# A hybrid decoder trunk on one core: the stick-breaking softplus through |z|, causal rows from the longest down, and memory heads that start after half of their queries

## The chip, the cores and the metric

The kernel runs on one core of one Trainium2 chip. The metric is device time in microseconds (us) of one execution; the times given are medians of several executions. A core has a matrix engine (PE, with its weight loads shown as PEld), a vector engine (DVE), a scalar engine (ACT), a general engine (POOL) and a queue engine (SP), which here issues the weight DMAs. Each engine works through its own instructions in order and waits on semaphores for the others.

## The reference

Two layers, each a half-step SwiGLU, a mixing block, and another half-step SwiGLU, with RMSNorm around each. The sequence has 512 rows of width 1024, and the memory has 256 rows. What matters here is the mixing block:

```python
# stick-breaking attention, 8 heads of width 64; z = q k^T / 8, mask: key < query
log_beta = log_sigmoid(z)
log_not = where(mask, log_beta - z, 0.0)              # = -softplus(z)
log_between = cumsum(log_not, reverse=True) - log_not
w = where(mask, exp(log_beta + log_between), 0.0)
o_sb = w @ v
# forgetting attention, 8 heads of width 64; c = cumsum(log_sigmoid(f_logit + b))
p = softmax(where(key <= query, z + c_query - c_key, -inf)); o_fx = p @ v
# memory attention, 4 heads of width 128
o_mem = softmax(q_mem k_mem^T * 128 ** -0.5) @ v_mem
merged = sigmoid(u@Wg_sb)*(o_sb@W_sb) + sigmoid(u@Wg_fx)*(o_fx@W_fx) + sigmoid(u@Wg_mem)*(o_mem@W_mem)
h = h + rmsnorm(merged @ w_out)
```

## The kernel before

Activations are kept transposed, as tiles of 128 features by 512 rows. Every float32 operand of a large product is split into a high part (an ACT copy that rounds) and a low part (a DVE subtraction), and `mm3` (L180 to L184) issues three matmuls: high by high, high by low, low by high. Weights arrive by DMA in a `raw` tile and are split the same way.

Work for PE comes from two kinds of source. The first is a queue of jobs, `Q`: each job is one projection or gate product, and its weights are loaded and split ahead of it. `Q.step(limit)` runs the next piece of the running job (three matmuls), and begins a new job only if its number is below the limit. `Q.until(n)` calls `step(n)` until it returns nothing, so it finishes a job that is already running, whatever its number. The second source are the heads, written as generators: a head issues its score matmuls, then yields `("wait", W)`, a guess of how long its softmax takes on ACT and DVE, then issues its transposes, yields another wait, and then issues the product with the values. `Q.weave(chain, limit)` keeps an assumed clock and fills the assumed waits with steps of jobs below the limit. When no job below the limit is left, the chain's next part follows at once and PE waits for the softmax itself. The framework's scheduler may still move single instructions within an engine's order.

In a layer's mixing block the jobs stand in this order before the change: memory queries 0 and 1 (`q_mem(0)`, tiles `qm` 0 and 1), memory queries 2 and 3 (`q_mem(1)`), then for the pairs of heads of the stick-breaking branch (p = 0 to 3) and of the forgetting branch (2, 3, 0, 1): `project` of the next pair (values `pv` for every second pair, queries `pq`, keys `pk`) and a `merge` job (gate product `pg`, branch product `pb`, a sigmoid on ACT and DVE). `run` finishes both memory queries, then weaves the four memory heads (scores `zm`, transposes `ptm`, values `pvm`) up to the mark `marks[0, 0]`, that is with the jobs `pv`, `pq` and `pk` of pair 0. Each memory head's scores are issued ahead of the previous head's transposes, and the wait between them is dropped. Then every pair of a branch gives two heads (j = 0 and 1), each woven up to the merge job of its pair, `marks["m", br, p]`.

A stick-breaking head (`stick_head`, scores `zs`, transposes `pts`, values `pvs`) works on four query blocks, i = 0 to 3, with 128, 256, 384 and 512 keys. For each it takes exp, a minimum with 2^62, and ln(1 + .) in `log1p_exp` (L170 to L172), then max(z, .) (L892), a reversed running sum (L894), a subtraction (L895) and exp (L896). The first transposes, `pts ... _0`, read all four blocks. A forgetting head (`zf`, `ptf`, `pvf`) does max, exp, reciprocal and a multiply per block. `forget_cumsum` (its transposes: `pfl`) makes the running sum of the forget gates once per layer.

Of the kernel before, what the change touches and what calls it, by code (L numbers as in the profile page):

```python
# [12 lines left out]
AF = mybir.ActivationFunctionType  # L13
ALU = mybir.AluOpType
# [3 lines left out]
P = 128  # L18
# [4 lines left out]
def kernel(  # L23
# [38 lines left out]
    nc = tc.nc  # L62
    _, S, D = x.shape
    M = mem.shape[1]
    L = w_in.shape[0]
    NT = S // P
    ND = D // P
    MT = M // P
    HD = 64
    NP = 4  # L70
    NH = 8
    HEAD_ROWS = ((slice(0, HD), slice(HD, P), 0), (slice(HD, P), slice(0, HD), 1))
    NMH = 4
# [94 lines left out]
    def log1p_exp(t, z, bias=0.0):  # L168

        nc.scalar.activation(t, z, AF.Exp, bias=bias)  # L170
        nc.vector.tensor_scalar(t, t, 2.0 ** 62, None, ALU.min)
        nc.scalar.activation(t, t, AF.Ln, bias=one_t[:t.shape[0]])  # L172
# [156 lines left out]
    def wpair(src, ktiles, c0, name, scale=None):  # L329

        return [Unit(src, k, min(4, ktiles - k), c0, 256, f"{name}_{k}", scale) for k in range(0, ktiles, 4)]
# [542 lines left out]

    def stick_head(q, k, vts, pj, j, ot, name):

        ptile = []
        pzs = [pbank("z", f"z{name}_{i}") for i in range(NT)]
        for i, pz in enumerate(pzs):
            nc.tensor.matmul(pz[:, i * P:(i + 1) * P], ident16[:], strict16, start=True, stop=False,  # L880
                             skip_group_check=True)
        for i, pz in enumerate(pzs):
            w = (i + 1) * P
            wp = max(w, 256)
            qs = slice(i * P, (i + 1) * P)
            for kk in (j, 2 + j):
                nc.tensor.matmul(pz[:, :wp], q[:, j, qs], k[:, kk, :wp], start=False, stop=(kk == 2 + j),
                                 skip_group_check=True)
            zr, t = pz[:, :w], tmp(f"t{name}_{i}")

            log1p_exp(t[:, :w], zr)
            nc.vector.tensor_tensor(t[:, :w], zr, t[:, :w], ALU.max)  # L892
            back = t[:, w - 1::-1]
            nc.vector.tensor_tensor_scan(back, one_t[:].broadcast_to([P, w]), back, 0.0, ALU.mult, ALU.add)  # L894
            nc.vector.tensor_tensor(t[:, :w], zr, t[:, :w], ALU.subtract)  # L895
            nc.scalar.activation(t[:, :w], t[:, :w], AF.Exp)  # L896
            ptile.append(t)
        yield ("pe", 1.5)
        yield ("wait", W_SB0)
        wt = transposed(ptile, name)  # L900
        yield ("pe", 1.1)
        yield ("wait", W_SB1)
        attend(pbank("mm", "pv" + name), j, vts, pj, wt, ot, name)
        yield ("pe", 1.2)
# [12 lines left out]
    def fox_head(q, k, vts, pj, j, qk, ot, name, ahead):  # L917

        rc = slice(0, 104 if j == 0 else P)
        ptile = []  # L920
        pzs = [pbank("z", f"z{name}_{i}") for i in range(NT)]
        for i, pz in enumerate(pzs):
            nc.tensor.matmul(pz[:, i * P:(i + 1) * P], ident16[:], causal16, start=True, stop=False,
                             skip_group_check=True)
        for i, pz in enumerate(pzs):
            w = (i + 1) * P
            wp = max(w, 256)
            qs = slice(i * P, (i + 1) * P)
            nc.tensor.matmul(pz[:, :wp], q[:, j, qs], k[:, j, :wp], start=False, stop=False, skip_group_check=True)
            nc.tensor.matmul(pz[:, :wp], qk[rc, 0, qs], qk[rc, 1, :wp], start=False, stop=True, skip_group_check=True)  # L930
            st = sb.tile([P, 2], F32, tag="st", bufs=8, name=f"st{name}_{i}")
            nc.vector.tensor_reduce(st[:, 0:1], pz[:, :w], AX.X, ALU.max, negate=True)
            p = tmp(f"p{name}_{i}")
            nc.scalar.activation(p[:, :w], pz[:, :w], AF.Exp, bias=st[:, 0:1], accum_out=st[:, 1:2])
            nc.vector.reciprocal(st[:, 1:2], st[:, 1:2])
            nc.vector.tensor_scalar(p[:, :w], p[:, :w], st[:, 1:2], None, ALU.mult)
            ptile.append(p)
        yield ("pe", 1.5)
        yield ("wait", W_FX0)
        tri = transposed(ptile, name)  # L940
        yield ("pe", 1.1)
        yield ("wait", W_FX1)
        ahead()
        attend(pbank("mm", "pv" + name), j, vts, pj, tri, ot, name)
        yield ("pe", 1.2)
# [73 lines left out]
    def mixing(l, src, ks, vs, dst):  # L1019
# [41 lines left out]
        def proj(key, un, scale):  # L1061
# [8 lines left out]
            else:  # L1070
# [3 lines left out]
                for r, ro, j in HEAD_ROWS:  # L1074
# [3 lines left out]
                    else:  # L1078
                        nc.gpsimd.tensor_copy(t[ro, j], t[r, j])

        def project(br, p):
            base = br * 1536
            if (br, p) == (1, FOX[0]):
                un = [Unit(w_in[l], k, min(3, ND - k), base + 1024 + p * P, 2 * P + NH, f"v{l}_{br}_{p}_{k}")
                      for k in range(0, ND, 3)]
                Q.add(un, lambda: v_gates(br, p // 2, un))
            elif p % 2 == 0:
                un = wpair(w_in[l], ND, base + 1024 + p * P, f"v{l}_{br}_{p}")
                Q.add(un, lambda: v_half(br, p // 2, un))
            for x, off, scale in (("q", 0, 0.125), ("k", 512, None)):  # L1090
                un1 = Unit(w_in[l], 0, ND, base + off + p * P, P, f"{x}{l}_{br}_{p}")
                marks[br, p] = Q.add([un1], lambda x=x, un1=un1, scale=scale: proj((x, br, p), un1, scale))
                if (br, p, x) == (1, FOX[0], "q"):
                    Q.add([], lambda: forget_cumsum(l, st["fl"], st))

        def merge(br, w_br, dp):

# [28 lines left out]

        for c in range(2):
            un = wpair(w_in[l], ND, 3080 + c * 256, f"qm{l}_{c}")
            marks["first"] = Q.add(un, lambda c=c, un=un: q_mem(c, un), src.ready(range(NT)) if c == 0 else None)
        project(0, 0)  # L1130
        heads = [(0, p) for p in range(NP)] + [(1, p) for p in FOX]
        for i, (br, p) in enumerate(heads):
            if i + 1 < len(heads):
                project(*heads[i + 1])
            marks["m", br, p] = merge(*((2, w_br_mem, i % NP) if br == 0 else (0, w_br_sb, i % NP)))
        for dp in range(ND // 2):
            merge(1, w_br_fox, dp)

# [9 lines left out]
        def run():  # L1148
            Q.until(marks["first"])
            for i in range(NT):  # L1150
                nc.sync.dma_start(hsave[i], hT[i][:])
            st["o", 2] = [blk("o", f"om{l}_{i}") for i in range(NMH)]

            def mems():
                gens = [mem_head(st["qm"][i], ks, vs, i, st["o", 2][i], f"m{l}_{i}") for i in range(NMH)]

                def part(g):
                    for kind, us_ in g:
                        yield (kind, us_)
                        if kind == "wait":  # L1160
                            return
                yield from part(gens[0])
                for i in range(NMH):
                    if i + 1 < NMH:
                        yield from ((k_, u_) for k_, u_ in part(gens[i + 1]) if k_ == "pe")
                    yield from gens[i]

            Q.weave(mems(), marks[0, 0])
            fx = {}
            for br in range(2):  # L1170
                st["o", br] = [blk("o", f"o{l}_{br}_{p}") for p in range(NP)]
                for at, p in enumerate(FOX if br else range(NP)):
                    Q.until(marks[br, p])
                    q, k = st["q", br, p], st["k", br, p]
                    vt = st["v", br, p // 2]
                    for j in range(2):
                        nm = f"{'sf'[br]}{l}_{p}_{j}"
                        ot = st["o", br][p]
                        if br == 0:
                            head = stick_head(q, k, vt, p % 2, j, ot, nm)  # L1180
                        else:
                            def pre(at, j):

                                if j == 2:
                                    at, j = at + 1, 0
                                p = FOX[at] if at < NP else None
                                if (p, j) not in fx and ("k", br, p) in st:
                                    fx[p, j] = fox_pre(st["q", br, p], st["k", br, p], j, 2 * p + j, st["cs"], f"{l}_{p}_{j}")

                            pre(at, j)  # L1190
                            head = fox_head(q, k, vt, p % 2, j, fx[p, j], ot, nm, lambda at=at, j=j: pre(at, j + 1))
                        Q.weave(head, marks["m", br, p])
                Q.until(marks["m", br, FOX[-1] if br else NP - 1])

        marks["run"] = run
        return marks
# [84 lines left out]
```

## Time and profile before

| | |
|---|---|
| median of 3 runs | 2488.55 us (2482.97 to 2490.67) |
| profiled execution, its own time | 2486.44 us |
| its span, first to last instruction | 2484.3 us |
| PE busy | 2441.4 us, 98% |
| DVE busy | 1542.6 us, 62% |
| ACT busy | 1143.5 us, 46% |
| mean granted PE clock | 0.996 |

Busy time of an engine is the time in which an instruction of it runs; for PE, consecutive matmuls overlap. Idle time of PE is what is left, and it is put down to what ended it. In the profile, tile names carry no numbers: `ts` is the softplus tile of any stick-breaking head, `pts` the transposes of any. The two layers' mixing blocks lie at about 400 to 835 us and 1632 to 2067 us of the span.

### The profile page before, as it was taken

Reading aid. Unit: us, or ns where it says so; the run is one execution under the profiler, and the core shown is the slowest. Engines: PE = TensorE matmul, PEld = TensorE weight load, DVE = VectorE, ACT = ScalarE, POOL = GpSimd, SP = SyncE. Lnnn points to the kernel's source line nnn. Section 1 sums busy time; section 2 is a strip of 40 time slices with the busy share of each in tenths; the row PEclk is TensorE's granted clock in tenths of the full one; section 3 lists DMA queues with packets and bytes.
Section 4 is the critical chain, followed back from the end, with each engine's and each line's share of the span. In section 5 each row is a group of like instructions: output and inputs, shape, how many; then the busy total and the mean of one; then the engine's idle time right before and its main releaser. Section 6 shows DMA issues by size and latency. Waiting matters only on the chain.

```text
span 2484.3 us, 30885 instructions
## 1 busy us (share of the span) xinstructions
PE 2441.4 (98%) x12154; PEld 2066.2 (83%) x12154; DVE 1542.6 (62%) x2259; ACT 1143.5 (46%) x1875; POOL 76.9 (3%) x124
## 2 busy tenths in 40 slices
PE   7999999999999999999999999999999999999998
PEld 7888889888888888888888888898888888888887
DVE  4364666778776544556643646768787765436465
ACT  4333355666555433333433333446675554333333
POOL 0000000000110000000000000000001100000000
PEclk9999999999999999999999999999999999999999
DMA  5343334122222523432423333442222224233332
GB/s 178 102 136 119 108 138 145 53 83 72 76 77 77 184 85 106 131 123 94 161 85 111 126 126 116 137 137 63 69 68 85 77 95 160 88 108 126 127 102 102
DMA packets 233298, 270.53 MB, mean 109 GB/s; under 512 B 8361, under 2 KB 188609, under 8 KB 233153
## 3 DMA queue, kind: packets, MB, share of 16 engines
q1 hardware_dynamic: 233056, 268.53, 33.7%
q8 instruction: 95, 1.56, 0.3%
q14 instruction: 51, 0.41, 0.0%
q0 software_dynamic: 96, 0.03, 0.0%
HBM read 262.24 MB, written 6.29 MB: 108 GB/s over the span
## 4 chain that ended last, share of the span: by engine, by line
PE 84%; DVE 8%; ACT 4%; DMA 2%; issue 1%; SPq 0%; DVEq 0%; ACTq 0%
PE pgc L183 3%; PE pgc L184 3%; PE pgc L182 3%; PE puc L183 3%; PE puc L184 3%; PE puc L182 3%; PE pga L183 3%; PE pga L184 3%; PE pga L182 3%; PE pua L184 3%; PE pua L183 3%; PE pua L182 3%; PE pg L182 3%; PE pg L184 3%; PE pg L183 3%; PE pdc L183 2%
## 5 line engine op out<-in xcount | busy, mean ns | idle before, releaser
L182 PE MATMUL pg<-us_a,wh_wg 128*128 128x512 f32 x384 | 150.4, 392 | 0.0
L184 PE MATMUL pg<-us_a,wl_wg 128*128 128x512 f32 x384 | 149.7, 390 | 0.0
L183 PE MATMUL pg<-us_a,wh_wg 128*128 128x512 f32 x384 | 149.6, 390 | 0.0
L182 PE MATMUL puc<-us_b,wh_uc 128*128 128x512 f32 (+1 forms) x384 | 142.6, 372 | 2.3 <-DVE fb L492 2.3
L184 PE MATMUL puc<-us_b,wl_uc 128*128 128x512 f32 (+1 forms) x384 | 142.4, 371 | 0.0
L183 PE MATMUL puc<-us_b,wh_uc 128*128 128x512 f32 (+1 forms) x384 | 142.4, 371 | 0.0
L182 PE MATMUL pgc<-us_b,wh_gc 128*128 128x512 f32 x320 | 124.5, 389 | 0.0
L183 PE MATMUL pgc<-us_b,wh_gc 128*128 128x512 f32 x320 | 124.5, 389 | 0.0
L184 PE MATMUL pgc<-us_b,wl_gc 128*128 128x512 f32 x320 | 124.5, 389 | 0.0
L163 DVE TENSOR_TENSOR wl_uc<-raw_uc,wh_uc 128x1024 fp32r<-128x1024 f32 x44 | 53.9, 1225 | 105.5 <-ACT wh_uc L162 105.5
L163 DVE TENSOR_TENSOR wl_ua<-raw_ua,wh_ua 128x1024 fp32r<-128x1024 f32 x44 | 53.9, 1225 | 96.5 <-ACT wh_ua L162 96.5
L163 DVE TENSOR_TENSOR wl_ga<-raw_ga,wh_ga 128x1024 fp32r<-128x1024 f32 x40 | 49.0, 1224 | 67.8 <-ACT wh_ga L162 67.8
L162 ACT CAST wh_uc<-raw_uc 128x1024 fp32r<-128x1024 f32 x44 | 46.3, 1052 | 92.5 <-PE pgc L183 39.4
L163 DVE TENSOR_TENSOR wl_gc<-raw_gc,wh_gc 128x1024 fp32r<-128x1024 f32 x40 | 48.9, 1223 | 63.4 <-ACT wh_gc L162 63.4
L184 PE MATMUL pda<-wh_da,ala 128*128 128x512 f32 x224 | 87.1, 389 | 0.0
L182 PE MATMUL pda<-wh_da,aha 128*128 128x512 f32 x224 | 87.1, 389 | 0.0
L183 PE MATMUL pda<-wl_da,aha 128*128 128x512 f32 x224 | 87.1, 389 | 0.0
L182 PE MATMUL pdc<-wh_dc,ahc 128*128 128x512 f32 x224 | 87.1, 389 | 0.0
L183 PE MATMUL pdc<-wl_dc,ahc 128*128 128x512 f32 x224 | 87.1, 389 | 0.0
L184 PE MATMUL pdc<-wh_dc,alc 128*128 128x512 f32 x224 | 87.1, 389 | 0.0
L162 ACT CAST wh_ga<-raw_ga 128x1024 fp32r<-128x1024 f32 x40 | 42.1, 1053 | 96.3 <-PE pua L183 76.3
L162 ACT CAST wh_ua<-raw_ua 128x1024 fp32r<-128x1024 f32 x44 | 46.2, 1051 | 86.7 <-PE pga L183 35.8
(437 smaller groups left out, 7285.6 us busy)
## 6 DMA issues: line engine op xcount, KB each, us to landing
raw_da<-in_ffn_w_down_dram SPq DMA_DIRECT2D x52, 512.0 KB, 3.3
raw_dc<-in_ffn_w_down_dram SPq DMA_DIRECT2D x52, 512.0 KB, 3.2
raw_wg<-in_w_gate_dram SPq DMA_DIRECT2D x48, 512.0 KB, 3.5
raw_ga<-in_ffn_w_gate_dram SPq DMA_DIRECT2D x44, 512.0 KB, 3.6
raw_ua<-in_ffn_w_up_dram SPq DMA_DIRECT2D x44, 512.0 KB, 3.6
raw_gc<-in_ffn_w_gate_dram SPq DMA_DIRECT2D x44, 512.0 KB, 3.6
raw_uc<-in_ffn_w_up_dram SPq DMA_DIRECT2D x44, 512.0 KB, 3.6
bta<-in_ffn_w_down_dram SPq DMA_DIRECT2D x16, 512.0 KB, 4.6
```

Source lines behind the costliest of these rows:

```text
L162: nc.scalar.copy(h_ap, src)
L163: nc.vector.tensor_tensor(l_ap, src, h_ap.bitcast(F32), ALU.subtract)
L182: nc.tensor.matmul(pt, lh, rh, start=start, stop=False, skip_group_check=free)
L183: nc.tensor.matmul(pt, lh, rl, start=False, stop=False, skip_group_check=free)
L184: nc.tensor.matmul(pt, ll, rh, start=False, stop=stop, skip_group_check=free)
```

## The change

Four things are changed in the mixing block. The softplus of a stick-breaking head becomes max(z, 0) + ln(1 + exp(-|z|)): ACT takes the absolute value, the exponential with scale -1 and the logarithm in a row, and DVE takes max and sum in one instruction; the minimum is gone. Both kinds of causal head issue and process their query blocks from i = 3 (512 keys) down to i = 0. The memory heads are woven in from the moment the first pair of memory queries is projected; each head asks, by `Q.until`, for the job with its own queries. And the value projections become jobs of their own, `project_v`, that stand behind the merge job of the pair two places earlier; a pair of heads may use all jobs up to the queries and keys of the pair after the next (`limits`), no longer only up to its own merge.

```diff
     def stick_head(q, k, vts, pj, j, ot, name):
-        for i, pz in enumerate(pzs):
+        for i in reversed(range(NT)):
+            pz = pzs[i]
...
-            log1p_exp(t[:, :w], zr)
-            nc.vector.tensor_tensor(t[:, :w], zr, t[:, :w], ALU.max)
+            nc.scalar.activation(t[:, :w], zr, AF.Abs)
+            nc.scalar.activation(t[:, :w], t[:, :w], AF.Exp, scale=-1.0)
+            nc.scalar.activation(t[:, :w], t[:, :w], AF.Ln, bias=one_t[:])
+            nc.vector.scalar_tensor_tensor(t[:, :w], zr, 0.0, t[:, :w], ALU.max, ALU.add)
...
     def fox_head(q, k, vts, pj, j, qk, ot, name, ahead):
-        for i, pz in enumerate(pzs):
+        for i in reversed(range(NT)):
+            pz = pzs[i]
...
+        def project_v(br, p):
+            base = br * 1536 + 1024 + p // 2 * 2 * P
+            if (br, p) == (1, FOX[0]):
+                un = [...]
+                Q.add(un, lambda: v_gates(br, p // 2, un))
+                Q.add([], lambda: forget_cumsum(l, st["fl"], st))
+            else:
+                un = wpair(w_in[l], ND, base, f"v{l}_{br}_{p}")
+                Q.add(un, lambda: v_half(br, p // 2, un))
         def project(br, p):
-            (the values' jobs)
+            marks["before", br, p] = len(Q.jobs)
             for x, off, scale in (("q", 0, 0.125), ("k", 512, None)):
                 marks[br, p] = Q.add([un1], lambda ...: proj((x, br, p), un1, scale))
-                if (br, p, x) == (1, FOX[0], "q"):
-                    Q.add([], lambda: forget_cumsum(l, st["fl"], st))
...
-            marks["first"] = Q.add(un, lambda c=c, un=un: q_mem(c, un), ...)
-        project(0, 0)
+            marks["qm", c] = Q.add(un, lambda c=c, un=un: q_mem(c, un), ...)
+        marks["first"] = marks["qm", 0]
+        project_v(*heads[0])
+        project(*heads[0])
-        for i, (br, p) in enumerate(heads):
+        for i, (br, _) in enumerate(heads):
             if i + 1 < len(heads):
                 project(*heads[i + 1])
-            marks["m", br, p] = merge(...)
+            merge(...)
+            if i % 2 == 0 and i + 2 < len(heads):
+                project_v(*heads[i + 2])
+        limits = [marks["before", *h] for h in heads[2:]] + 2 * [len(Q.jobs)]
...
             def mems():
+                def head(i):
+                    Q.until(marks["qm", i // 2])
+                    return mem_head(st["qm"][i], ks, vs, i, st["o", 2][i], f"m{l}_{i}")
...
+                gen = head(0)
+                yield from part(gen)
                 for i in range(NMH):
                     if i + 1 < NMH:
-                        yield from ((k_, u_) for k_, u_ in part(gens[i + 1]) if k_ == "pe")
-                    yield from gens[i]
+                        following = head(i + 1)
+                        yield from ((k_, u_) for k_, u_ in part(following) if k_ == "pe")
+                    yield from gen
+                    gen = following
...
-                        Q.weave(head, marks["m", br, p])
-                Q.until(marks["m", br, FOX[-1] if br else NP - 1])
+                        Q.weave(head, limits[br * NP + at])
+            Q.until(limits[-1])
```

More of the change, by code (lines that the diff above doesn't have):

```diff
@@ L875, in stick_head @@
     def stick_head(q, k, vts, pj, j, ot, name):
-        ptile = []
+        ptile = {}
         pzs = [pbank("z", f"z{name}_{i}") for i in range(NT)]
@@ L896, in stick_head @@
             nc.scalar.activation(t[:, :w], t[:, :w], AF.Exp)
-            ptile.append(t)
+            ptile[i] = t
         yield ("pe", 1.5)
@@ L919, in fox_head @@
         rc = slice(0, 104 if j == 0 else P)
-        ptile = []
+        ptile = {}
         pzs = [pbank("z", f"z{name}_{i}") for i in range(NT)]
@@ L936, in fox_head @@
             nc.vector.tensor_scalar(p[:, :w], p[:, :w], st[:, 1:2], None, ALU.mult)
-            ptile.append(p)
+            ptile[i] = p
         yield ("pe", 1.5)
@@ L1079, in proj @@
                         nc.gpsimd.tensor_copy(t[ro, j], t[r, j])
+        def project_v(br, p):
+            base = br * 1536 + 1024 + p // 2 * 2 * P
+            if (br, p) == (1, FOX[0]):
+                un = [Unit(w_in[l], k, min(3, ND - k), base, 2 * P + NH, f"v{l}_{br}_{p}_{k}")
+                      for k in range(0, ND, 3)]
+                Q.add(un, lambda: v_gates(br, p // 2, un))
[3 more added lines that the diff above has]
+                Q.add(un, lambda: v_half(br, p // 2, un))
         def project(br, p):
             base = br * 1536
[L1083 to L1089, printed above, removed]
+            marks["before", br, p] = len(Q.jobs)
             for x, off, scale in (("q", 0, 0.125), ("k", 512, None)):
@@ L1128, in mixing @@
             un = wpair(w_in[l], ND, 3080 + c * 256, f"qm{l}_{c}")
-            marks["first"] = Q.add(un, lambda c=c, un=un: q_mem(c, un), src.ready(range(NT)) if c == 0 else None)
-        project(0, 0)
+            marks["qm", c] = Q.add(un, lambda c=c, un=un: q_mem(c, un), src.ready(range(NT)) if c == 0 else None)
+        marks["first"] = marks["qm", 0]
         heads = [(0, p) for p in range(NP)] + [(1, p) for p in FOX]
-        for i, (br, p) in enumerate(heads):
+        project_v(*heads[0])
+        project(*heads[0])
+        for i, (br, _) in enumerate(heads):
             if i + 1 < len(heads):
                 project(*heads[i + 1])
-            marks["m", br, p] = merge(*((2, w_br_mem, i % NP) if br == 0 else (0, w_br_sb, i % NP)))
+            merge(*((2, w_br_mem, i % NP) if br == 0 else (0, w_br_sb, i % NP)))
+            if i % 2 == 0 and i + 2 < len(heads):
+                project_v(*heads[i + 2])
+        limits = [marks["before", *h] for h in heads[2:]] + 2 * [len(Q.jobs)]
         for dp in range(ND // 2):
@@ L1154, in mems @@
             def mems():
-                gens = [mem_head(st["qm"][i], ks, vs, i, st["o", 2][i], f"m{l}_{i}") for i in range(NMH)]
+                def head(i):
+                    Q.until(marks["qm", i // 2])
+                    return mem_head(st["qm"][i], ks, vs, i, st["o", 2][i], f"m{l}_{i}")
                 def part(g):
@@ L1161, in part @@
                             return
-                yield from part(gens[0])
+                gen = head(0)
+                yield from part(gen)
                 for i in range(NMH):
                     if i + 1 < NMH:
-                        yield from ((k_, u_) for k_, u_ in part(gens[i + 1]) if k_ == "pe")
-                    yield from gens[i]
+                        following = head(i + 1)
+                        yield from ((k_, u_) for k_, u_ in part(following) if k_ == "pe")
+                    yield from gen
+                    gen = following
             Q.weave(mems(), marks[0, 0])
```

## The prediction

> **What bounds the kernel now.** I read the page first, then PE's waits in the first mixing block, then that block cut at each place where PE stops.
>
> ```profile
> span 2484.3 us, 30885 instructions
> ...
> PE 2441.4 (98%) x12154; PEld 2066.2 (83%) x12154; DVE 1542.6 (62%) x2259; ACT 1143.5 (46%) x1875; POOL 76.9 (3%) x124
> ```
>
> PE is the bound: it idles 2484.3 - 2441.4 = 42.9 us in all. The built program of the changed kernel has the same 12154 matmuls in the same sizes, so the change can only move PE's stalls, and only in the two mixing blocks. The next view is busy time by stretch (us, then PE, PEld, DVE, ACT, POOL, granted PE clock), with its own total, for the first layer, and one stretch of the second.
>
> ```profile
> 458.00:467.00 9.00, 6.95 (x32) 5.13 (x32) 7.13 (x14) 5.01 (x14) 2.56 (x4) 0.81 0.21 60
> ...
> 498.00:504.00 6.00, 5.49 (x37) 4.45 (x36) 4.41 (x9) 4.29 (x10) 0.21 (x1) 1.00 0.50 159
> 504.00:533.00 29.00, 29.00 (x182) 26.18 (x181) 24.85 (x47) 19.22 (x39) 0.20 (x1) 1.00 0.22 64
> 533.00:536.00 3.00, 1.69 (x13) 1.35 (x12) 2.25 (x4) 1.78 (x4) 1.03 (x1) 1.00 0.48 143
> ...
> 582.00:589.00 7.00, 6.61 (x45) 5.32 (x43) 4.61 (x9) 4.46 (x10) 0.20 (x1) 1.00 0.55 157
> ...
> 617.00:620.00 3.00, 2.28 (x16) 1.84 (x15) 2.97 (x5) 1.59 (x4) 0.41 (x1) 1.00 0.00 0
> ...
> 774.00:776.00 2.00, 1.09 (x7) 0.77 (x6) 1.67 (x2) 2.00 (x6) 0.00 (x0) 1.00 0.78 257
> ...
> sum 422.00, PE 415.97 PEld 356.14 DVE 314.81 ACT 250.05 POOL 37.08; mean PE 32.00 PEld 27.40 DVE 24.22 ACT 19.23 POOL 2.85
> ...
> 1690.00:1699.00 9.00, 7.13 (x33) 5.45 (x31) 7.46 (x16) 5.24 (x12) 2.36 (x3) 0.81 0.19 59
> ```
>
> From 413 to 835 us PE idles 422.00 - 415.97 = 6.03 us, nearly all in the six places shown; the second layer repeats the first (1.87 us in the stretch that answers to the first row, 2.05 us there). The first row also shows a clock of 0.81, a loss of 9 x 0.19 = 1.7 us. So all there is to win is about 2 x (6.0 + 1.7) = 15.4 us, 0.6% of the time. The rows below say what ends each stop.
>
> ```profile
> 453.83 0.28 PE L184 MATMUL zm<-mk,qm 128*128 128x256 f32 x1
> 453.95 1.04 PE L978 MATMUL ptm<-ident,pm 128*128 128x128 f32 x8
> 454.75 0.48 PE L182 MATMUL pk<-us_a,wh_k 128*128 128x512 f32 x1
> ...
> 456.92 0.39 PE L182 MATMUL pvm<-ptm,mv 128*128 128x512 f32 x1
> ...
> 458.29 0.60 PE L978 MATMUL ptm<-ident,pm 128*128 128x128 f32 x4
> ...
> 460.27 0.44 PE L978 MATMUL ptm<-ident,pm 128*128 128x128 f32 x2 [1.28 <-DVE pm L969]
> 461.31 0.44 PE L978 MATMUL ptm<-ident,pm 128*128 128x128 f32 x2 [0.60 <-DVE pm L969]
> ...
> 462.37 0.79 PE L182 MATMUL pvm<-ptm,mv 128*128 128x512 f32 x1 [0.17 <-ACT ptm L162]
> ...
> 499.33 0.50 PE L858 MATMUL pvs<-pts,v 128*128 128x512 f32 x1 [0.51 <-ACT pts L162]
> ...
> 532.83 0.39 PE L184 MATMUL pg<-us_a,wl_wg 128*128 128x512 f32 x1
> 533.06 0.49 PE L871 MATMUL pts<-ident,ts 128*128 128x128 f32 x3
> 534.86 0.88 PE L871 MATMUL pts<-ident,ts 128*128 128x128 f32 x6 [1.31 <-ACT ts L896]
> ...
> 584.34 0.67 PE L858 MATMUL pvs<-pts,v 128*128 128x512 f32 x2 [0.29 <-DVE pts L163]
> ...
> 619.09 0.98 PE L871 MATMUL pts<-ident,ts 128*128 128x128 f32 x7 [0.72 <-ACT ts L896]
> ...
> 775.43 0.50 PE L858 MATMUL pvf<-ptf,v 128*128 128x512 f32 x1 [0.91 <-ACT ptf L162]
> ```
>
> Four kinds. At the **end of the memory heads** the queue below the limit is empty, and PE waits for the last head's softmax (1.28 + 0.60 + 0.17). In stick heads 1/1 and 3/1 (pair/j) the **last exp comes late** (1.31, 0.72). After heads 0/1 and 2/1 the merge's last three matmuls are all that covers the **split of the transposes** (the stretches at 498 and 582: 0.51 and 0.39). The end of the last forgetting head costs 0.91.
>
> **The change, part by part**, per layer.
>
> *Memory heads, +2.0 us.* At first sight the new weave gives them 48 more matmuls (`pqm` 2 and 3, 2 x 24). But each new head calls `Q.until`, which finishes whatever job is running. The order of the built program shows it: all 48 stand between the first head's scores and the second's, where the old order had 57 shorter ones (`pv`); then the rest of `pv` (39) is finished ahead of the third head's scores, and the rest of `pk` (18) ahead of the fourth's. So the queue is empty earlier: old, nine `pk` matmuls stand between the third head's transposes and its `pvm`; new, none do. In the rows, those nine run from 454.75 to 456.92, 2.17 us. The wait they cover is from the last score matmul (453.83) to the last `ptm` (461.31), 7.48 us, and its ACT and DVE work (max, exps, multiplies, the split of `ptm`, a gate weight, the keys) is the same in the new order. Take away 2.17 us of cover and PE idles 2.17 us more, part of it now ahead of `pvm`. I take +2.0. Ends: +0.5 if the key and weight splits, which now partly run earlier, shorten the wait; +3.9 if a second span of half clock (1.7) joins.
>
> *Softplus and row order: the late exps, 0.* The groups of all lines give the price of each step.
>
> ```profile
> L894 DVE TENSOR_TENSOR_SCAN ts<-one_t,ts 128x128 f32<-128x128 f32 (+1 forms) x64 | 50.0, 806 | 0.3
> ...
> L172 ACT ACTIVATE ts<-ts,one_t 128x128 f32<-128x128 f32 (+1 forms) x64 | 32.5, 555 | 5.0 <-DVE ts L171 4.8
> ...
> L896 ACT ACTIVATE ts<-ts 128x128 f32<-128x128 f32 (+1 forms) x64 | 30.1, 470 | 31.2 <-DVE ts L895 30.2
> ...
> L892 DVE TENSOR_TENSOR ts<-zs,ts 128x128 f32<-128x128 f32 (+1 forms) x64 | 28.9, 477 | 0.7 <-ACT ts L172 0.5
> ...
> L895 DVE TENSOR_TENSOR ts<-zs,ts 128x128 f32<-128x128 f32 (+1 forms) x64 | 28.8, 475 | 0.3
> ...
> L170 ACT ACTIVATE ts<-zs 128x128 f32<-128x128 f32 (+1 forms) x64 | 24.8, 436 | 1.2 <-PE zs L887 0.9
> ...
> L171 DVE TENSOR_SCALAR ts<-ts 128x128 f32<-128x128 f32 (+1 forms) x64 | 18.3, 317 | 0.5
> ```
>
> Removed: 64 minima, 18.3 us of DVE, and two crossings between ACT and DVE per block. Added: 64 absolute values, which no row shows; the nearest is L170, which reads the same scores (24.8 us), and the bounds are 18.3 (L171) and 32.5 us (L172). The exp now reads SBUF as L896 does (30.1 for 24.8), and the fused max and sum I price as L892. Per head (16 of them): ACT (24.8 + 32.5 + 30.1) / 16 = 5.5 becomes 7.3 us; DVE (18.3 + 28.9 + 50.0 + 28.8) / 16 = 7.9 becomes 6.7. In the row 504:533 DVE is busy 86% and ACT 66%, so the load goes from the fuller engine to the emptier one. All of this lies beside PE's matmuls; what counts is when the last exp is ready. Longest first, the last block is the short one, so less follows it, but the first transpose now needs it, while before only the fourth did (the row at 533.06 shows three going ahead).
>
> The program's order tells more. In the old order the matmuls that stand between a head's last exp and its `pts` are 17, 6, 19, 2, 8, 8, 16, 3 for heads 0/0 to 3/1; PE waits at those with 2 and 3, and at no other. In the new order they are 7, 6, 8, 6, 2, 11, 3, 10: again one 2 and one 3, at heads 2/0 and 3/0. I take the same price in the new places: 0 net. Ends: -2.0 (both gone: 1.31 + 0.72) and +2.0 (two more such heads).
>
> Here the Trainium skill speaks against the change: "ScalarE: Activation LUTs", section "Rules for kernel authors", wants maximum and the like on VectorE and not on ScalarE. The trace agrees on the price of one: 317 ns for the DVE minimum against 436 ns for the nearest ACT row. By that rule the swap would lose 64 x 0.119 = 7.6 us of engine time.
>
> *Value projections and limits, -0.7 us.* The limit of pairs 0 and 2 now takes in the following `pv` job, so their second heads get 33 `pv` matmuls ahead of `pvs` (old: three `pb`). The stops at 498 and 582 go, 0.90 us. In return pairs 1 and 3 end at their merge: three and six `pb` matmuls are left there. The first is the old case again (about 0.45), the second half covered (0.2), partly filled by the scheduler. I take -0.7 with the slower starts around each stop; ends -1.5 and 0. The `pv` weights are fetched and split one pair earlier on SP, ACT and DVE; no row shows PE waiting for a weight here, and the order of weights is otherwise kept. The `pfl` transposes move from head 3/1 to 3/0, behind the first block's subtraction as before: 0 to +0.5.
>
> *Forgetting heads, +0.4 us.* Same instructions, the long block first. Between the last multiply and the first `ptf` the order has 4 matmuls at heads 2/0 and 1/0 and 1 at 1/1 (old: 9, 5 and 0, but there the first three transposes could go ahead), so PE may stop briefly where it doesn't now. 0 to +1.2.
>
> Sum per layer: +2.0 + 0 - 0.7 + 0.4 = +1.7, twice +3.4. The profiled execution's own time is 2486.44 us (span 2484.3 and 2.1 around it), which makes 2489.8; it lies 2.1 us under the median of the runs, 2488.55. Set on the median: 2492.0 us.
>
> **Rivals.** *ACT becomes the bound of the stick heads* (slower). ACT's chain grows by 1.9 us a head. It decides where fewer than about nine matmuls (2 us) follow the last exp: six heads of eight. At half of 1.9 us in each, 2 x 6 x 0.94 = 11.3 us, which with the rest (+3.4) is 2503. For: these engines are in-order, and weight splits and sigmoids share them. Against: 66% against 86% above. By the rule of the Trainium skill quoted above this is how it goes. *The late exps go and the memory tail hardly grows* (small gain): 2 x (-2.0 - 0.7 + 0.4 + 0.5) = -3.6, 2485. For: two crossings and the DVE step less. *The tail shrinks so far that the half clock goes too* (faster): 2 x (-2.0 - 1.5 - 1.0 - 1.7) = -12.4, 2476. Against: the order, which empties the queue sooner. "TensorE: Matmul & The Clock Gate", Part 1, in the Trainium skill, has the clock judged in free-running windows of 3413 ns; 1.7 us lost at half rate is such a window, and the trace agrees. *The stalls only change places*: 2488.5.
>
> **How the numbers follow.** 0.3% is 7.5 us, about what a measurement of this kernel can tell from no change. My forecast (2492) has 0.45, stalls that only change places 0.13, the small gain 0.12, ACT as the bound 0.22, the fast case 0.08. The forecast's own upper end, with second half-clock spans in both layers, passes 2496: I move 0.04 of its chance there. Faster 0.08, same 0.66, slower 0.26. The range goes from 2482, between the small gain and the fast case (ends -2.0, -1.5, 0, +0.5 twice: -6.0), to 2503.
>
> **What would show it.** In the changed profile: PE idle ahead of `pvm` and the last `ptm` about 4 us per layer instead of 2.05; no `pvs` stop after heads 0/1 and 2/1; waits on the last exp at 2/0 and 3/0 and none at 1/1 and 3/1; ACT some 30 us busier, DVE some 18 us less. I am wrong if PE's waits on `ts` grow beyond 4 us a layer (ACT), or if the memory tail idles less than now.

## The result, and the profile after

| | before | changed |
|---|---|---|
| median, 22 runs each | 2486.45 us (2482.61 to 2490.76) | 2491.03 us (2488.12 to 2495.06) |
| ratio, 95% interval | | 1.0017 (1.0012 to 1.0023) |
| profiled execution, its own time | 2486.44 us | 2490.06 us |
| its span | 2484.3 us | 2487.9 us |

The change costs 0.17%, about 4.2 us (3.0 to 5.7), against a forecast of +3.4 us. The page of the changed kernel:

```profile
span 2487.9 us, 30833 instructions
...
PE 2443.4 (98%) x12154; PEld 2066.1 (83%) x12154; DVE 1525.5 (61%) x2195; ACT 1163.1 (47%) x1939; POOL 77.3 (3%) x124
```

PE's 12154 matmuls are the same, DVE is 17.1 us less busy and ACT 19.6 us more. Busy time by stretch (us; PE, PEld, DVE, ACT, POOL; granted clock; then the DMA engines' share and GB/s), the first layer and one stretch of the second:

```profile
454.00:465.00 11.00, 8.15 (x38) 6.75 (x37) 8.40 (x18) 6.28 (x16) 2.27 (x3) 0.69 0.17 48
...
545.00:549.00 4.00, 3.80 (x20) 2.56 (x19) 3.31 (x6) 3.69 (x8) 0.00 (x0) 1.00 0.66 209
...
561.50:564.50 3.00, 1.91 (x13) 1.37 (x12) 2.94 (x7) 2.37 (x6) 0.00 (x0) 1.00 0.00 0
...
603.00:611.00 8.00, 7.25 (x38) 5.54 (x37) 7.31 (x14) 4.37 (x10) 1.60 (x1) 1.00 0.50 133
...
617.00:620.00 3.00, 1.75 (x12) 1.42 (x11) 2.89 (x7) 0.77 (x2) 0.71 (x2) 1.00 0.56 178
...
774.00:778.00 4.00, 3.28 (x19) 2.40 (x18) 3.53 (x9) 3.67 (x9) 0.00 (x0) 1.00 0.43 131
...
sum 422.00, PE 415.06 PEld 354.57 DVE 304.51 ACT 257.74 POOL 37.13; mean PE 31.93 PEld 27.27 DVE 23.42 ACT 19.83 POOL 2.86
...
1690.00:1702.00 12.00, 9.15 (x49) 7.68 (x49) 8.58 (x18) 7.00 (x16) 2.27 (x3) 0.86 0.16 44
```

PE idles 422.00 - 415.06 = 6.94 us where it idled 6.03. At the end of the memory heads it is 2.85 us instead of 2.05, at a clock of 0.69 in the first layer: two half-clock spans, a loss of at most 11 x 0.31 = 3.4 us (part of them falls on idle time), before it was one. Over whole executions the clock does not explain the 4.2 us: the mean granted clock of the changed kernel's 22 runs is 0.9962, and that of the kernel before, in the three sets of 24 to 33 runs made beside the experiments, 0.9957 to 0.9960. The two profiled executions have five half-clock spans of 3.41 us each ahead of their last 15 us. The rows of PE say what ended each stop:

```profile
454.57 0.28 PE L184 MATMUL zm<-mk,qm 128*128 128x256 f32 x1
454.69 1.04 PE L983 MATMUL ptm<-ident,pm 128*128 128x128 f32 x8
456.02 0.50 PE L182 MATMUL pvm<-ptm,mv 128*128 128x512 f32 x1 [0.29 <-ACT ptm L162]
459.08 0.80 PE L183 MATMUL pvm<-ptm,mv 128*128 128x512 f32 x1 [2.56 <-DVE ptm L163]
...
462.34 1.06 PE L983 MATMUL ptm<-ident,pm 128*128 128x128 f32 x4
...
563.73 0.98 PE L871 MATMUL pts<-ident,ts 128*128 128x128 f32 x7 [1.09 <-ACT ts L900]
...
609.97 1.20 PE L871 MATMUL pts<-ident,ts 128*128 128x128 f32 x9 [0.53 <-ACT ts L900]
...
618.54 0.62 PE L858 MATMUL pvs<-pts,v 128*128 128x256 f32 x3 [1.25 <-DVE pts L163]
...
775.70 1.28 PE L871 MATMUL ptf<-ident,pf 128*128 128x128 f32 x10 [0.60 <-DVE pf L941]
```

The nine `pk` matmuls between the third `ptm` and its `pvm` are gone, and PE stands 2.56 us in front of the second `pvm` matmul until DVE has split the transposes. DVE is late with that split because the splits of a gate weight and of the new keys (and a maximum) stand ahead of it in its order. In the kernel before, the same split began 1.43 us after the start of the last `zm`, in the changed one 3.77 us after it; first the row of the kernel before, then those of the changed one:

```profile
455.26 0.69 DVE L163 TENSOR_TENSOR ptm<-ptm,ptm 128x512 fp32r<-128x512 f32 x1
```

```profile
454.89 1.23 DVE L166 SCALAR_TENSOR_TENSOR wl_wg<-raw_wg,wh_wg 128x1024 fp32r<-128x1024 f32 x1
456.04 0.68 DVE L163 TENSOR_TENSOR k<-pk,k 64x512 fp32r<-64x512 f32 x1
...
457.41 0.69 DVE L163 TENSOR_TENSOR k<-pk,k 64x512 fp32r<-64x512 f32 x1
...
458.34 0.69 DVE L163 TENSOR_TENSOR ptm<-ptm,ptm 128x512 fp32r<-128x512 f32 x1
```

The last group of `ptm` then starts without a wait. Heads 2/0 and 3/0 wait for their last exp (1.09, 0.53), 1/1 and 3/1 no longer do, and the stops of 0.5 us for `pvs` after 0/1 and 2/1 are gone. A stop of 1.25 us within `pvs` of head 3/0 is new. It ends with the split of the last transposes, and ahead of that split DVE works through `forget_cumsum` (tiles `fa`, `fb`, `cs`) and a weight, 4.7 us in all; this running sum came one head later in the old order:

```profile
613.29 0.67 DVE L1015 TENSOR_TENSOR fa<-fb,fa 8x512 f32<-8x512 f32 x1
613.99 1.22 DVE L1016 TENSOR_TENSOR_SCAN fb<-one_t,fa 8x512 f32<-8x512 f32 x1
615.13 1.19 DVE L163 TENSOR_TENSOR wl_q<-raw_q,wh_q 128x1024 fp32r<-128x1024 f32 x1
616.35 1.68 DVE L1021 TENSOR_TENSOR cs<-fb,cs 8x512 fp32r<-8x512 f32 x2
618.07 0.62 DVE L163 TENSOR_TENSOR pts<-pts,pts 128x256 fp32r<-128x256 f32 x2
```

### The profile page after: what moved, and what is told of

It reads as the page before. It is cut to its first block, busy times and chain, and to the rows that moved or that the text cites. A ratio compares the mean times of both kernels' runs of the same rounds, so it can differ in the third digit from the quotient of the medians.

```text
span 2487.9 us, 30833 instructions
## 1 busy us (share of the span) xinstructions
PE 2443.4 (98%) x12154; PEld 2066.1 (83%) x12154; DVE 1525.5 (61%) x2195; ACT 1163.1 (47%) x1939; POOL 77.3 (3%) x124
## 4 chain that ended last, share of the span: by engine, by line
PE 85%; DVE 7%; ACT 4%; DMA 3%; issue 1%; SPq 0%; DVEq 0%; ACTq 0%
PE puc L183 3%; PE puc L184 3%; PE puc L182 3%; PE pgc L183 3%; PE pga L183 3%; PE pgc L182 3%; PE pga L182 3%; PE pg L184 3%; PE pgc L184 3%; PE pg L183 3%; PE pg L182 3%; PE pga L184 3%; PE pua L182 3%; PE pua L184 3%; PE pua L183 3%; PE pdc L183 2%
```

## The experiments

Two theories stood at the start. A: PE's stops decide, and `Q.until` in the new memory heads takes their cover away. B: ACT's longer chain in the stick heads is the loss. Each part was run alone on the kernel before; memory, softplus and row order were then left out of the changed kernel one by one; and the call of `Q.until` was mended. The ratios of the experiments (7 to 11 runs each) are to runs of the kernel before made beside them, with medians of 2485.43 to 2485.93 us, not to the 2486.45 in the first row; differences given below in us are differences of these ratios. The last column is read from the starts of matmuls in each trace: the stretch from the first `pqm` matmul to the last `pb` of the forgetting branch, in layer 1 and layer 2, and in brackets how many half-clock spans of 3.41 us (at most 1.7 us lost in each) lie in it.

| run | median us | ratio to before, 95% | mixing stretch, us |
|---|---|---|---|
| before | 2486.45 | 1 | 440.4, 440.3 (1, 1) |
| changed | 2491.03 | 1.0017 (1.0012 to 1.0023) | 443.4, 442.1 (2, 1) |
| mem_only | 2489.07 | 1.0016 (1.0007 to 1.0025) | 440.1, 440.0 (0, 0) |
| softplus_only | 2490.13 | 1.0021 (1.0013 to 1.0030) | 442.5, 442.2 (1, 1) |
| order_only | 2488.84 | 1.0015 (1.0006 to 1.0024) | 440.0, 441.6 (0, 1) |
| values_only | 2485.12 | 0.9997 (0.9988 to 1.0006) | 439.8, 438.5 (1, 0) |
| softplus_and_order | 2492.83 | 1.0026 (1.0016 to 1.0036) | 444.3, 442.7 (1, 0) |
| all_but_memory | 2488.82 | 1.0010 (1.0001 to 1.0019) | 441.3, 441.2 (1, 1) |
| all_but_softplus | 2492.75 | 1.0026 (1.0017 to 1.0036) | 444.7, 443.7 (2, 1) |
| all_but_order | 2487.51 | 1.0005 (0.9996 to 1.0013) | 440.5, 439.3 (1, 0) |
| until_mended | 2481.68 | 0.9986 (0.9977 to 0.9995) | 438.5, 438.4 (0, 0) |
| mended_memory_only | 2480.18 | 0.9979 (0.9970 to 0.9989) | 437.8, 437.7 (0, 0) |
| values_and_mended_memory | 2482.16 | 0.9986 (0.9977 to 0.9995) | 438.4, 437.3 (1, 0) |
| mended_all_but_order | 2478.42 | 0.9972 (0.9961 to 0.9983) | 436.7, 436.8 (0, 0) |

### One part at a time

mem_only, on the kernel before:

```diff
+        marks["first"] = marks["qm", 0]
...
+                def head(i):
+                    Q.until(marks["qm", i // 2])
+                    return mem_head(st["qm"][i], ks, vs, i, st["o", 2][i], f"m{l}_{i}")
...
```

> Memory heads alone changed (Q.until in each new head, start after half of the queries); softplus, row order, values and limits as before. Theory A (the call of Q.until burns the cover, and this is what makes the changed kernel slower): PE waits about 2.6 us for the low part of ptm ahead of the third pvm in each layer, the stick heads' waits stay as before (1.31 and 0.72 us on the last exp at heads 1/1 and 3/1), and the kernel is slower by 2 x 2 = 4 us, up to 6 with one more half-clock span, ratio 1.0016 to 1.0024. Theory B (the loss comes from ACT in the stick heads, the new weave gives the memory heads more cover): same or faster, ratio 0.998 to 1.000.

softplus_only:

```diff
-            log1p_exp(t[:, :w], zr)
-            nc.vector.tensor_tensor(t[:, :w], zr, t[:, :w], ALU.max)
+            nc.scalar.activation(t[:, :w], zr, AF.Abs)
+            nc.scalar.activation(t[:, :w], t[:, :w], AF.Exp, scale=-1.0)
+            nc.scalar.activation(t[:, :w], t[:, :w], AF.Ln, bias=one_t[:])
+            nc.vector.scalar_tensor_tensor(t[:, :w], zr, 0.0, t[:, :w], ALU.max, ALU.add)
```

> Only the softplus changed (Abs, Exp, Ln on ACT, max and sum in one on DVE). Theory A: the stalls only change places; the program's order has the last exp 2 to 4 matmuls ahead of pts at heads 1/0, 2/0 and 3/0 and no longer at 1/1 and 3/1, so 0 to 1 us per layer either way: ratio 0.9995 to 1.0005. Theory B (ACT is the bound): waits on the last exp grow to over 4 us a layer, ratio 1.002 or more. ACT busier by 20 to 30 us, DVE less by about 18 us in both.

order_only, in both kinds of causal head:

```diff
-        for i, pz in enumerate(pzs):
+        for i in reversed(range(NT)):
+            pz = pzs[i]
```

> Only the order of the query blocks changed (512 keys first) in both kinds of causal head. Theory A: waits on the last exp move from heads 1/1 and 3/1 (2.0 us together) to 0/0, 2/0 and 3/0 (about 1.5 us together), and the forgetting heads get 0.4 to 0.6 us of waits for ptf per layer: ratio 0.9997 to 1.0006. Theory B: neutral as well. A third theory (long rows first shortens the chain, as the edit suggests): no waits on the last exp at all, 2 x 2 us faster, ratio 0.9984.

values_only, with `project_v` as in the whole change:

```diff
+            if i % 2 == 0 and i + 2 < len(heads):
+                project_v(*heads[i + 2])
...
+        limits = [marks["before", *h] for h in heads[2:]] + 2 * [len(Q.jobs)]
...
-                        Q.weave(head, marks["m", br, p])
+                        Q.weave(head, limits[br * NP + at])
```

> Only the place of the value projections and the limits of the pairs changed; memory heads, softplus and row order as before. Theory A: the stops for pvs after heads 0/1 and 2/1 go (1.0 us together by idle time) and smaller ones come after 1/1 and 3/1; the order has no head with fewer than four matmuls between the last exp and pts, so the waits on the last exp (2.0 us) go too: 1 to 2.5 us less per layer, ratio 0.998 to 0.9992. Theory B (the edit is neutral, all comes from ACT): ratio 0.9996 to 1.0004.

Three of the four parts cost when done alone, 3.7 to 5.2 us each by the ratios, and they do not add up: the sum of the four ratios is +0.49%, the whole change +0.17%. mem_only came out as theory A has it: 1.0016, and the same wait of 2.6 us per layer for the low part of `ptm`. softplus_only went against my expectation and the way of theory B. Its waits for `pts`:

```profile
515.56 0.66 PE L871 MATMUL pts<-ident,ts 128*128 128x128 f32 x4 [0.44 <-DVE ts L897]
517.03 0.65 PE L871 MATMUL pts<-ident,ts 128*128 128x128 f32 x4 [0.69 <-ACT ts L898]
...
564.02 0.98 PE L871 MATMUL pts<-ident,ts 128*128 128x128 f32 x7 [0.73 <-ACT ts L898]
...
600.87 0.66 PE L871 MATMUL pts<-ident,ts 128*128 128x128 f32 x4 [0.74 <-DVE ts L897]
602.34 0.66 PE L871 MATMUL pts<-ident,ts 128*128 128x128 f32 x4 [0.44 <-ACT ts L898]
```

That is 3.04 us in the heads 1/0, 2/0 and 3/0, for 2.03 us in 1/1 and 3/1 before: the right places, and 1 us a layer too much. It is short of the 4 us that theory B asked for, but the time, 1.0021, is what that theory forecast. In order_only the same three heads wait, and head 0/0 as well:

```profile
476.63 1.31 PE L871 MATMUL pts<-ident,ts 128*128 128x128 f32 x10 [0.51 <-ACT ts L897]
...
513.35 1.31 PE L871 MATMUL pts<-ident,ts 128*128 128x128 f32 x10 [0.34 <-ACT ts L897]
...
560.96 1.31 PE L871 MATMUL pts<-ident,ts 128*128 128x128 f32 x10 [0.91 <-ACT ts L897]
...
598.21 1.31 PE L871 MATMUL pts<-ident,ts 128*128 128x128 f32 x10 [0.45 <-ACT ts L897]
```

All ten transposes (x10) stand behind the wait, since the first one now reads the block that is done last. The four waits make 2.21 us, for 2.03 us before. The third theory, that the long block first shortens the chain, fell; the first was missed too, since the order costs 1.0015 where 1.0006 was its upper end. values_only, at 0.9997, came out neutral, as theory B has it, and not 1 to 2.5 us a layer faster. In it one wait for an exp is left, and the new stop at `pvs` of head 3/0 shows without any of the other parts, so it belongs to the values' new place, which takes `forget_cumsum` along:

```profile
562.61 0.98 PE L871 MATMUL pts<-ident,ts 128*128 128x128 f32 x7 [0.37 <-ACT ts L897]
...
617.78 0.62 PE L858 MATMUL pvs<-pts,v 128*128 128x256 f32 x3 [1.71 <-DVE pts L163]
```

### One part left out

all_but_memory is the changed kernel with the old weave of the memory heads:

```diff
-        marks["first"] = marks["qm", 0]
+        marks["first"] = marks["qm", 1]
...
-                def head(i):
-                    Q.until(marks["qm", i // 2])
-                    return mem_head(st["qm"][i], ks, vs, i, st["o", 2][i], f"m{l}_{i}")
-
+                gens = [mem_head(st["qm"][i], ks, vs, i, st["o", 2][i], f"m{l}_{i}") for i in range(NMH)]
...
```

> The changed kernel with the memory heads as before (both memory queries first, old weave); softplus, row order, values and limits as changed. Theory A (Q.until burns the cover of the memory heads): the wait ahead of the third pvm (2.6 us a layer) goes, the old waits for ptm (1.9 us a layer) come back, half-clock spans at the end of the memory heads get fewer: faster than the changed kernel by 2 to 4 us, ratio to the kernel before 1.0000 to 1.0009. Theory B (ACT in the stick heads is the whole loss): as the changed kernel, 1.0017.

all_but_softplus and all_but_order take the softplus hunk and the row order back out of the changed kernel (the diffs above, reversed); softplus_and_order leaves out memory and values.

> The changed kernel with the old softplus (exp, minimum, ln, max). If ACT's longer chain is what costs in the changed kernel (theory B, and the run of the softplus alone), it is faster than the changed kernel by 3 to 5 us: ratio to the kernel before 0.9997 to 1.0005. If the softplus costs only where the values stand in their old place (theory A), it is as the changed kernel within 1.5 us: 1.0011 to 1.0023.

> The changed kernel with the query blocks in the old order (128 keys first). If the row order costs here as it does alone (it cost about 1 us a layer in the first layer's and the second layer's stalls when done alone): 2 us faster than the changed kernel, ratio to the kernel before 1.0006 to 1.0012. If it pays together with the new softplus: 2 us slower than the changed kernel, 1.0022 or more. Places: the waits for ptf (0.75 us a layer at the last head) go and the wait for pvf there is 1.15 us again.

> Softplus and row order changed together, memory heads, values and limits as before. If their costs add up (each alone 1.0021 and 1.0015): 1.003 or more, over 3 us of stalls more per layer. If the order makes up for the softplus's longer chain on ACT, or the other way round: as one of them alone, 1.0010 to 1.0022, with waits on the last exp at heads 1/0, 2/0 and 3/0 as in both single runs.

Without the new memory weave the change costs 1.0010 instead of 1.0017, 1.7 us less, a little under what was expected; the intervals overlap. Without the softplus it costs more (1.0026), so beside the other three parts the softplus seems to pay, by some 2 us, where alone it cost 5: both of my readings for that run were wrong. The two intervals overlap, but the traces agree: PE idles 8.3 and 8.4 us in the two mixing stretches of all_but_softplus, 6.9 us in each of the changed kernel. Without the row order it costs 1.0005, a little under the range for an order that costs, with 6.0 us of idle time in each stretch, and these profile rows of all_but_order show part of why: three of the transposes go ahead again, and the wait at head 2/0 is 0.37 us, not 1.09.

```profile
561.40 0.55 PE L871 MATMUL pts<-ident,ts 128*128 128x128 f32 x3 [0.37 <-DVE ts L898]
...
615.70 0.62 PE L858 MATMUL pvs<-pts,v 128*128 128x256 f32 x3 [1.32 <-DVE pts L163]
```

softplus_and_order costs 1.0026 in the old place of the values and 1.0010 in the new (all_but_memory): the new place and limits are worth 4 us there, while alone they are worth nothing that shows. The 1.0026 lies between the two readings of its expectation: the costs neither add up in full nor make up for each other. The idle time agrees with the gain: 8.6 and 8.4 us in the stretches of the one, 6.0 and 5.9 us in those of the other. So theory B holds in part: with the values in their old place, ACT's longer chain does cost. In softplus_only the heads 1/0, 2/0 and 3/0 have their exps late; in softplus_and_order it is 2/0 and 3/0 (1.39 and 0.71 us, none at 1/0), with further stops ahead of `pfl` (1.30 us) and `pvs`. One difference in the traces is the cover: in head 1/0 the matmuls between the last scores and the first `pts` last 8.7 us in softplus_only and 10.9 us in all_but_memory. That this is the reason was not tested.

### The call of Q.until mended

```diff
                 def head(i):
-                    Q.until(marks["qm", i // 2])
+                    if len(st["qm"]) <= i:
+                        Q.until(marks["qm", i // 2])
```

> The changed kernel with one condition: a new memory head calls Q.until only if its queries are not projected yet, so a running job is not finished early. Theory A: the 33 us of jobs then cover the memory heads' waits to the end; PE's waits for ptm and ahead of pvm go, in both layers, with the half-clock span there; head 0/0 may wait up to 1 us for its last exp. Faster than the changed kernel by 2 x 3 to 2 x 5 us: ratio to the kernel before 0.9977 to 0.9993. Theory B: no faster than the changed kernel by more than 1 us, 1.0013 to 1.0017.

> Values and limits as changed, memory heads as changed with the same condition on Q.until; softplus and row order as before. Theory A with what the runs of the single parts showed (softplus and row order each cost, values neutral): the end of the memory heads without waits, so 2 x 3 to 2 x 4 us less than with the values alone: ratio 0.9965 to 0.9975, the fastest of all. If the softplus and the row order pay once the values stand in their new place, until_mended is faster than this one.

> Memory heads alone changed, with the condition on Q.until; all else as before. Theory A: the end of the memory heads has no waits, the stick heads' waits are those of the kernel before (1.31 and 0.72 us on the last exp, 0.5 us ahead of pvs), and head 0/0 waits up to 1 us: 1 to 2.5 us less per layer and fewer half-clock spans, ratio 0.9978 to 0.9992.

> The changed kernel with the condition on Q.until and the old order of query blocks: softplus, values and limits as changed. Theory A from the single parts: between until_mended and values_and_mended_memory or under both, 0.9980 to 0.9988, if the row order costs with the new softplus too; over until_mended (0.9986) by 1 to 2 us if the order pays together with the softplus.

This settles the memory heads: the call of `Q.until` is what empties the queue. One condition takes the changed kernel from 1.0017 (1.0012 to 1.0023) to 0.9986 (0.9977 to 0.9995), some 8 us by the ratios and as theory A had it. About half of it is idle time: 4.9 and 4.7 us in the two stretches, for 6.9 in each. The rest can be the clock, whose mean over the runs rises from 0.9962 to 0.9980, at most 4.5 us. One stretch, the end of the first layer's memory heads, in four profiles: the kernel before, the changed one, mem_only, until_mended.

```profile
454.00:466.00 12.00, 9.95 (x48) 7.84 (x46) 10.54 (x24) 7.80 (x20) 2.35 (x3) 0.86 0.16 45
```

```profile
454.00:466.00 12.00, 9.15 (x43) 7.56 (x42) 8.59 (x18) 6.28 (x16) 2.27 (x3) 0.72 0.16 45
```

```profile
454.00:466.00 12.00, 9.10 (x51) 7.03 (x49) 11.11 (x27) 8.58 (x23) 2.47 (x4) 1.00 0.16 45
```

```profile
454.00:466.00 12.00, 11.91 (x57) 9.50 (x57) 6.53 (x9) 6.52 (x12) 2.28 (x3) 1.00 0.29 89
```

PE is busy for 9.95, 9.15, 9.10 and 11.91 of 12 us. Mended, the idle time is 0.1 us and the clock full, and 57 matmuls get through where 43 did. Alone on the old kernel the mended weave gives 0.9979, as expected, and the lowest ratio is that of the changed kernel with the condition and the old row order: 0.9972 (0.9961 to 0.9983), 7 us under the kernel before and lower than was expected. The intervals of these two overlap, so it is not shown that the other parts add anything to the mended weave. values_and_mended_memory was expected to be the fastest, at 0.9965 to 0.9975; it missed that, with 0.9986, the same as until_mended. The pairs that differ in the row order alone agree: 1.0017 to 1.0005, and 0.9986 to 0.9972, 3 us each, though within each pair the intervals just overlap.

## Why the prediction was right, and where its terms were not

The time came out where it was forecast, +4.2 us (3.0 to 5.7) for +3.4 us, in the direction and by a mechanism named first. That mechanism is shown, but it is not the whole sum, and some of the agreement is luck. The terms were counted in idle time of PE, +1.7 us a layer; the traces have +0.9 and +1.1 us. In the first layer this is +0.8 us at the memory heads (forecast +2.0), -0.4 at the late exps (0), +0.5 at `pvs` (-0.7) and about -0.2 in the forgetting heads (+0.4). The mixing stretches of the two profiles grew by 3.0 and 1.8 us, at most 1.7 us of it in one more half-clock span; so 1 us or more at full clock is neither idle time nor clock, and where it goes is not shown. By its steps:

*PE bounds, and only its stalls move.* Right as to the work: the same 12154 matmuls. Idle time alone does not give the 4.2 us, as said.

*Memory heads, +2.0 a layer.* The mechanism is right and shown: the emptied queue, the place (`pvm` of the third head), and the cure. Alone it costs 4.0 us (1.0016, interval 1.7 to 6.2 us), just the two times 2.0; beside the other parts 1.7 us (1.0010 to 1.0017). The idle time itself was oversized: 2.85 us in place of about 4, all of it ahead of `pvm` and none at the last `ptm`. The step that was off is that the wait is the same in the new order. In mem_only, which has the same stop at full clock, it is 6.26 us from the last `zm` to the last group of `ptm`, where 7.48 us were taken over:

```profile
453.61 0.28 PE L184 MATMUL zm<-mk,qm 128*128 128x256 f32 x1
...
459.87 0.63 PE L978 MATMUL ptm<-ident,pm 128*128 128x128 f32 x4
```

DVE's work is the same, but in another order: the key and weight splits now come first, which delays the split of the third head's `ptm` and lets the fourth head's multiplies end sooner. Half clock at this place was in the forecast's upper end; it came as two spans in the first layer of the changed profile and one in the second, before one each. mem_only shows that it need not come: its profiled execution has none in either mixing block, and at 2482.53 us it was the fastest of its eleven runs. Its granted clock was 0.998, that of the other ten 0.995 to 0.997; a thousandth is 2.5 us.

*Softplus and row order, 0.* Right in the places and open in the net. The places were right, 2/0 and 3/0 with a wait and 1/1 and 3/1 without, and their price nearly so: 1.09 + 0.53 = 1.62 us for 2.03. But neither edit is free by itself. The order costs 3 us beside the other parts; the softplus pays some 2 us there and costs 5 alone, depending on where the values stand. The prediction says that the first transpose now needs the last block, and then counts matmuls ahead of `pts` as if the fourth still did. Both together, beside the moved values, come to 3.2 us with the old memory weave (values_only 0.9997, all_but_memory 1.0010) and to nothing with the mended one (both 0.9986), each with an uncertainty of some 3 us; with the values in their old place to 6.5 us. So the zero does not belong to the two edits; it depends on what stands beside them.

The prices of the instructions held: 24.8 us for the absolute values, as their nearest row had it:

```profile
L895 ACT ACTIVATE ts<-ts,one_t 128x512 f32<-128x512 f32 (+1 forms) x64 | 32.9, 557 | 0.1
...
L896 DVE SCALAR_TENSOR_TENSOR ts<-zs,ts 128x512 f32<-128x512 f32 (+1 forms) x64 | 28.8, 482 | 17.4 <-ACT ts L895 17.4
L900 ACT ACTIVATE ts<-ts 128x512 f32<-128x512 f32 (+1 forms) x64 | 28.6, 467 | 29.2 <-DVE ts L899 29.0
...
L894 ACT ACTIVATE ts<-ts 128x512 f32<-128x512 f32 (+1 forms) x64 | 27.2, 469 | 0.1
...
L893 ACT ACTIVATE ts<-zs 128x512 f32<-128x512 f32 (+1 forms) x64 | 24.8, 432 | 2.2 <-PE zs L889 1.8
```

The max and sum in one cost 28.8 us, for 28.9 of the maximum. ACT's four softplus rows make 113.5 us, where three made 87.4 us: 26.1 us more, for 30 forecast, mostly because the exp from SBUF cost 27.2 us and not 30.1. ACT as a whole grew by 19.6 us; what its other work lost was not followed up.

The quoted rule, maximum and its like on VectorE and not on ScalarE ("ScalarE: Activation LUTs" in the Trainium skill, "Rules for kernel authors"), would have the swap lose: alone it does, 1.0021; beside the other parts it seems not to. The price per instruction agrees (432 ns on ACT, 317 on DVE); what the kernel gains or loses differs with where the values stand.

*Values and limits, -0.7 a layer.* The stops at 0/1 and 2/1 went as foretold. The term that was too small is the move of `forget_cumsum` from head 3/1 to 3/0, put at 0 to +0.5 for its transposes: its work on DVE, ahead of the split for `pvs`, makes PE stand 1.25 us there (1.71 us in values_only). Alone the edit is neutral (0.9997), with softplus and order it is worth 4 us.

*Forgetting heads, +0.4.* Too much: 0.60 us for `ptf` at the last head in place of 0.91 for `pvf`, and about nothing at the others.

So in idle time the memory and forgetting terms were too large, the term of the values had the wrong sign, and the late exps fell a little; part of the agreement of the sum is that these errors cancelled, and part is lengthening that no term held.

## What to carry to other kernels

Where a bound engine's idle time is covered by a queue of other work, count the cover that is left at the end of the chain, not what was added at its start: 48 more matmuls made the end worse, because a call meant to wait for one job also finished whichever job was running. When jobs move, look at what moves with them on the helping engines: both new stops of the changed kernel end with a split that stood late in DVE's order. Parts of a change that share engines do not add up, so test them in their places (leave one out), not alone only. And when the rows of a block are reordered, look which row the first consumer reads.

## What the runs showed of the hardware

The matrix engine's half clock came in spans of 3.41 us, or two in a row, and each took at most 1.7 us. The spans of a trace all begin on one grid of 3.413 us, and the grid lies differently to the kernel's start in each execution (1.1 us after it in the kernel before, 2.4 us in mem_only). Laid on this grid, from 12 us after the start to 2468 us, the fourteen traces show how much idle time goes with a span. All 19 full-clock windows in which PE idled 1.89 us or more were followed by half clock; so were 28 of the 52 windows with 1.35 to 1.89 us, and none of the 3854 with less. The spans are not bound to the memory heads: the kernel before has others at 892, 1250 and 2124 us, and values_and_mended_memory one at 614.0 us, after the stop of 1.71 us at head 3/0.

So the same stop can cost a span or not. In mem_only's first layer the 2.9 us of idle time fell into two windows, 1.10 and 1.77 us, and the clock stayed at 1.00; in the changed kernel's second layer 2.56 of 2.85 us fell into one, and a span followed; in the kernel before 1.87 us in one were enough. Two profiles may thus differ by 2 us in nothing but this.
